# Two-part gather and weighting of expert tokens, with the adds moved behind the next block's first products

## The chip, the cores and the metric

One core of a Trainium2 chip runs the whole program. The metric is the device time of one execution in microseconds. Before the change three runs took 1808.55, 1808.65 and 1813.86 us, median 1808.65. A profile of one more execution (1807.88 us) was taken; all rows below are of that one.

## The reference

Two layers over 256 latent and 256 context tokens of width 1024. The change lies in the last stage, a mixture of experts over the 256 latent tokens, in float32 throughout:

```python
def moe_ffn(t, w_router, w1, w3, w2):
    logits = (t @ w_router).astype(jnp.float32)
    top_val, top_idx = lax.top_k(logits, TOP_K)
    gates = jax.nn.softmax(top_val, axis=-1)
    combine = jnp.sum(gates[..., None] * (top_idx[..., None] == jnp.arange(N_EXPERTS)), axis=-2)
    ...
    for e in range(N_EXPERTS):
        out = out + combine[..., e:e + 1] * swiglu(t, w1[e], w3[e], w2[e])
    return out
```

Each token takes two of eight experts (hidden width 3584). After it comes h = LayerNorm(sqrt(2) * h + mod5 * f), and that is the output.

## The kernel before, in words

The experts' stage is the last half of the program: from 878 us on the program loads 8 x 3 weight matrices, 352 MB, and ends some 20 us after the last of them. Tokens are sorted to experts on the chip. Experts are ranked by their number of tokens, and the rank fixes the room: 192, 128, 96, 96, 64, 32, 32 and 32 slots, 672 in all. `onehots` (L1467) builds two matrices G, 128 tokens x 672 slots, that hold 1 where a token sits in a slot. `gather` (L1491) multiplies the normalised rows n by G in two halves of 336 slots: for each of 8 feature blocks two float32 products, one for each half of the tokens; each result is scaled and shifted on its way out of PSUM and is the input xg of all experts. A float32 product appears in the trace as two records; a product of float32r operands, which `mm3` (L55) uses in the earlier stages, as one (a one-pass product in what follows). `split` (L49) makes such operands: ScalarE copies a tensor rounded to float32r, and VectorE subtracts the copy to get the rest.

The work is a list of jobs (`moe`, L1612): an expert's hidden width is cut in 7 chunks, and a chunk's slots in units of 128, 64 or 32 rows. `chunk_order` (L1582) interleaves chunks of large and of small experts. A job is `unit_hidden` (two products with the chunk's w1 and w3, then silu and product), `unit_turn` (a transpose, for units under 128 rows) and `unit_out` (the product with w2, added on VectorE to the unit's sum ya, tag "ya", 4 buffers). The order is `hidden(i)`, with the transposes of job i-1 inside it, then `out(i-1)`. Each chunk needs three loads of 2 MB, `wa`, `wb` and `wc` (L1602, L1605, L1608), from SyncE's queue into 7 buffers. A load waits in the queue until TensorE has finished with a buffer.

When an expert's last chunk is out, `unit_out` multiplies the sum by the row g5, `combine_matrix` (L1478) makes a slots x tokens matrix of gates (is-equal, times gate, transposed on TensorE, copied from PSUM at L1487), and `combine` (L1568) multiplies it with ya: four float32 products of 512 columns, each added to the residual rows K.res at L1576. There are 11 such units. The eleventh is of the expert that ends last; its last two chunks go through `ending` (L1679). The instructions of the loop are ordered by a planner that takes them in the program's order and moves ready ones forward on an idle engine; only `ending` and the router ahead of the stage stand in the written order. `overflow` (L1755) is a loop for tokens that found no slot; it runs zero times here. In `rest(0)` (L2154) two rows are spread over the partitions (L2147) and GpSimd makes K.res from n with them.

Of the kernel before, what the change touches and what calls it, by code (L numbers as in the profile page):

```python
# [1466 lines left out]
def onehots(K, pool, R):  # L1467
    nc = K.nc
    G = []
    for i in range(2):  # L1470
        G.append(pool.tile([128, NSLOT], F32, tag="ya", name="G", bufs=4))
        for r in range(NE):
            nc.vector.tensor_scalar(G[i][:, BASE[r]:BASE[r] + CAPS[r]], R.iota192[:, :CAPS[r]], R.pos[:, i, r:r + 1], None,
                                    op0=ALU.is_equal)
    return G


def combine_matrix(K, pool, R, kind, base, pos, gate, tag, bufs):  # L1478

    nc = K.nc  # L1480
    pt = K.bank()
    for i in range(2):
        t = pool.tile([128, 128], F32, tag="cmb_t", name="cmb_t", bufs=2)
        nc.vector.tensor_scalar(t, R.iot[(kind, base)], pos[:, i], gate[:, i], op0=ALU.is_equal, op1=ALU.mult)
        nc.tensor.transpose(pt[:, i * 128:(i + 1) * 128], t, K.ident)
    c = pool.tile([128, 256], F32, tag=tag, name="cmb", bufs=bufs)
    nc.vector.tensor_copy(c, pt[:, 0:256])  # L1487
    return c


def gather(K, n, G, lo, hi, xg, A, B):  # L1491
    nc = K.nc
    N = hi - lo
    for k in range(8):
        ps = K.bank()
        for i in range(2):
            nc.tensor.matmul(ps[:, :N], lhsT=n[i][:, k * 128:(k + 1) * 128], rhs=G[i][:, lo:hi], start=(i == 0), stop=(i == 1))  # L1497
        if k % 2:
            nc.scalar.activation(xg[:, k, lo:hi], ps[:, :N], AF.Identity, scale=A[:, k, 1:2], bias=B[:, k, 1:2])
        else:  # L1500
            nc.vector.tensor_scalar(xg[:, k, lo:hi], ps[:, :N], A[:, k, 1:2], B[:, k, 1:2], op0=ALU.mult, op1=ALU.add)
# [46 lines left out]
def unit_out(K, kind, gT, w2, ya, first, last):  # L1548
# [9 lines left out]
    for hf in range(2):  # L1558
# [3 lines left out]
        else:  # L1562
            K.nc.vector.tensor_tensor(ya[:, o], Y[hf], ya[:, o], op=ALU.add)  # L1563
        if last:
            K.nc.vector.tensor_tensor(ya[:, o], ya[:, o], K.g5[:, o], op=ALU.mult)  # L1565


def combine(K, c, ya):  # L1568

    nc = K.nc  # L1570
    for hf in range(2):
        o = slice(hf * 512, (hf + 1) * 512)
        for i in range(2):
            ps = K.bank()
            nc.tensor.matmul(ps, lhsT=c[:, i * 128:(i + 1) * 128], rhs=ya[:, o], start=True, stop=True)  # L1575
            nc.vector.tensor_tensor(K.res[i][:, o], ps, K.res[i][:, o], op=ALU.add)  # L1576


# [33 lines left out]
def moe(K, pool, R, G, n, A, B, rest):  # L1612
    nc = K.nc
    xg = pool.tile([128, 8, NSLOT], F32, tag="xg", name="xg")
    e = {}
    gather(K, n, G, 0, NSLOT // 2, xg, A, B)
    gather(K, n, G, NSLOT // 2, NSLOT, xg, A, B)
    ya = {}
    jobs = []

    def hidden(j, between=None):
# [10 lines left out]
    def out(j):  # L1632
        key = j["r"], j["u"]
        final = 4 if j["r"] == jobs[-1]["r"] else 6
        if j["ch"] == 0:
            ya[key] = pool.tile([128, D], F32, tag="ya", name="ya", bufs=4)
        if j["ch"] == final:
            r = j["r"]
            c = j["c"] = combine_matrix(K, pool, R, j["kind"], j["base"], R.pos[:, :, r:r + 1], R.gate[:, :, r:r + 1], "cmb", 2)
        unit_out(K, j["kind"], j["gT"], j["w"][2], ya[key], j["ch"] == 0, j["ch"] == final)  # L1640
        if j["ch"] == final:
            combine(K, c, ya.pop(key))

# [8 lines left out]
    for i in range(n - 2):  # L1652
        hidden(jobs[i], (lambda: turn(jobs[i - 1])) if i else None)
        if i:
            out(jobs[i - 1])
# [3 lines left out]
    turn(jobs[n - 3])  # L1659
    out(jobs[n - 3])  # L1660
    hidden(jobs[n - 2])
    return turn, hidden, jobs[n - 2:], jobs[n - 3]["c"]
# [91 lines left out]

def overflow(K, pool, R, n, A, B, end, nov):  # L1755
    nc = K.nc
    with K.tc.For_i(0, nov) as i:
# [4 lines left out]
        for t in range(2):  # L1762
            nc.vector.tensor_scalar(Gt[t], R.iot[(128, 0)], col[:, t:t + 1], None, op0=ALU.is_equal)
        xg = pool.tile([128, 8, 128], F32, tag="xg", name="ovx")
        gather(K, n, Gt, 0, 128, xg, A, B)
        c = combine_matrix(K, pool, R, 128, 0, col[:, 0:2, None], col[:, 2:4, None], "cmb", 2)
        ya = pool.tile([128, D], F32, tag="ya", name="ya", bufs=4)
        for ch in range(7):
            wa, wb, wc = load_chunk(K, e, ch)
            unit_out(K, 128, unit_hidden(K, pool, 128, xg, wa, wb)[0], wc, ya, ch == 0, ch == 6)  # L1770
        combine(K, c, ya)
        end()
# [21 lines left out]
def hybrid_block(ctx, tc, a, out, dbg=None, stop=None):  # L1794
# [30 lines left out]
    K.ph31 = cst.tile([128, 2, 64], F32, tag="ph31", name="ph31")  # L1825
    K.q_d = tc.dram_tile([16, 128, 240], F32, name="q_d")

    lnp = ctx.enter_context(tc.tile_pool(name="lnp", bufs=1))
# [150 lines left out]
    with tc.tile_pool(name="lat", bufs=1) as lp:  # L1979
# [10 lines left out]
        else:  # L1990
            n = latter(K, L, G, nn, lnp, sp, lp1, lp, ps, h[2:], g5)
    rn = ctx.enter_context(tc.tile_pool(name="rn", bufs=1))
    n2 = [rn.tile([128, D], F32, tag="n%d" % i, name="n") for i in range(2)]
# [142 lines left out]
    with tc.tile_pool(name="moew", bufs=1) as mw:  # L2136
        G = onehots(K, mw, R)

        row = [mo.tile([128, D], F32, tag="row%d" % i, name="row") for i in range(3)]

# [13 lines left out]
        def rest(i):  # L2154

            if i == 0:
                spread(0, row[0], ALPHA)
                spread(1, row[1], ALPHA)
# [14 lines left out]
        with tc.manual_schedule(engines=ALL):  # L2173
            ending(K, lnp, *lastly, row, out)
        overflow(K, mw, R, n, A2, B2, end, nov)

# [97 lines left out]
```

## Time and profile before

| | before |
|---|---|
| median of three runs | 1808.65 us |
| the profiled execution: its time, its span | 1807.88 us, 1806.0 us |
| TensorE busy, mean granted clock | 1690.3 us (94%), 0.970 |
| VectorE, ScalarE, GpSimd busy | 833.7, 408.8, 295.6 us |
| gather (L1497), 64 records | 882.2 to 902.3 us |
| combine products (L1575), 88 records | first at 1074.4, last at 1769.6 us |
| weight load queue | 509.5 MB, 73.6% of the 16 DMA engines' span |

Times in rows are microseconds from the start of the span, mean durations in ns. PE is TensorE's matmul, PEld its weight load, DVE is VectorE, ACT ScalarE, POOL GpSimd, SPq SyncE's queue. Matmuls overlap, so one record's duration is longer than the step from one to the next.

### The profile page before, as it was taken

The numbers are of one execution on the slowest core, as the hardware profiler recorded it, in microseconds if no ns is written. First come the engines' busy times: TensorE is split into PE (matmuls) and PEld (weight loads), VectorE is DVE, ScalarE is ACT, GpSimd is POOL, SyncE is SP. The second block draws the span as 40 slices with busy tenths as digits, with TensorE's granted clock in tenths as the row PEclk, the third lists the DMA queues.
The fourth block names the chain that finished last, engine by engine and source line by source line (L and its number), as shares of the span: only waits on it lengthen the run. The fifth ranks groups of instructions, "written<-read, shape, count | busy, mean of one in ns | idle before, by whom it ended". The sixth has DMA issues, their size and how long they took to land.

```text
span 1806.0 us, 34633 instructions
## 1 busy us (share of the span) xinstructions
PE 1690.3 (94%) x14673; PEld 1172.7 (65%) x14673; DVE 833.7 (46%) x1480; ACT 408.8 (23%) x775; POOL 295.6 (16%) x433
## 2 busy tenths in 40 slices
PE   6999997998999999559899999999999999999996
PEld 3755576776777777448576767666667665555553
DVE  2755559849987578994502121114011131241244
ACT  2555543222222464434210000000000001001001
POOL 7910005034542000563020000000000000000000
PEclk9999999999999999769989999999999999999998
DMA  8478762379996776868699799998999998999995
GB/s 322 163 244 264 260 193 92 117 201 283 308 301 220 251 250 200 252 170 311 279 400 401 312 400 396 427 426 351 373 426 396 397 390 327 427 426 376 390 388 212
DMA packets 96119, 556.29 MB, mean 308 GB/s; under 512 B 15128, under 2 KB 25052, under 8 KB 71128
## 3 DMA queue, kind: packets, MB, share of 16 engines
q1 hardware_dynamic: 78240, 509.52, 73.6%
q0 software_dynamic: 17536, 43.91, 8.4%
q8 instruction: 118, 1.93, 0.4%
q10 hardware_dynamic: 184, 0.59, 0.1%
q14 instruction: 41, 0.34, 0.1%
HBM read 529.41 MB, written 24.54 MB: 307 GB/s over the span
## 4 chain that ended last, share of the span: by engine, by line
PE 57%; DVE 6%; issue 2%; ACT 1%; POOL 1%; DMA 0%; ACTq 0%; DVEq 0%; POOLq 0%
PE bank L1526 18%; PE bank L1555 14%; PE bank L1517 11%; PE bank L57 2%; PE bank L58 2%; PE bank L59 2%; PE bank L1575 2%; PE bank L1497 1%; PE bank L1543 1%; DVE sG L1122 1%; PE bank L2147 1%; DVE su L1213 1%; ACT whl L51 0%; DVE ya L1563 0%; DVE ya L1565 0%
## 5 line engine op out<-in xcount | busy, mean ns | idle before, releaser
L1555 PE MATMUL bank<-wc,mgT 128*32 128x512 f32 (+2 forms) x1200 | 265.2, 598 | 0.5 <-DVE mgT L44 0.5
L1531 ACT ACTIVATE msl<-bank 128x128 f32<-128x128 f32 (+2 forms) x77 | 28.8, 374 | 730.9 <-PE bank L1526 558.9
L52 DVE TENSOR_TENSOR whl<-wraw,whl 128x1024 fp32r<-128x1024 f32 (+3 forms) x126 | 150.6, 1198 | 76.0 <-ACT whl L51 74.0
L1526 PE MATMUL bank<-wa,xg 128*32 128x128 f32 (+1 forms) x3136 | 173.7, 308 | 0.0
L59 PE MATMUL bank<-u,whl 128*128 128x512 f32 (+1 forms) x416 | 164.4, 395 | 9.6 <-DVE whl L52 9.6
L1526 PEld LDWEIGHTS bank<-wa,xg 128*32 128x32 f32 (+1 forms) x3136 | 125.9, 119 | 72.1 <-PE bank L1555 18.7
L1555 PEld LDWEIGHTS bank<-wc,mgT 128*32 128x32 f32 (+2 forms) x1200 | 85.6, 134 | 131.8 <-issue 127.2
L1526 PE MATMUL bank<-wb,xg 128*32 128x128 f32 (+1 forms) x3136 | 170.5, 304 | 0.0
L57 PE MATMUL bank<-u,whl 128*128 128x512 f32 (+1 forms) x416 | 166.6, 400 | 3.9 <-DVE u L52 3.9
L51 ACT CAST whl<-wraw 128x1024 fp32r<-128x1024 f32 (+3 forms) x126 | 125.6, 998 | 174.9 <-PE bank L59 142.5
L58 PE MATMUL bank<-u,whl 128*128 128x512 f32 (+1 forms) x416 | 163.7, 393 | 0.0
L1563 DVE TENSOR_TENSOR ya<-bank,ya 128x512 f32<-128x512 f32 x128 | 88.4, 690 | 139.4 <-PE bank L1555 139.2
L1532 DVE TENSOR_TENSOR msg<-msl,bank 128x128 f32<-128x128 f32 (+1 forms) x63 | 21.8, 347 | 270.9 <-PE bank L1526 270.9
L1526 PEld LDWEIGHTS bank<-wb,xg 128*32 128x32 f32 (+1 forms) x3136 | 122.2, 117 | 37.6 <-issue 3.7
L1746 POOL TENSOR_TENSOR y<-y,row 128x512 f32<-128x512 f32 x2 | 3.0, 1507 | 877.4 <-ACT y L1745 877.4
L1517 PEld LDWEIGHTS bank<-xg,wa 128*128 128x128 f32 x896 | 103.2, 194 | 9.0 <-PE bank L1555 6.0
L1517 PE MATMUL bank<-xg,wa 128*128 128x128 f32 x896 | 104.8, 279 | 0.0
L1517 PE MATMUL bank<-xg,wb 128*128 128x128 f32 x896 | 102.3, 275 | 0.0
L1517 PEld LDWEIGHTS bank<-xg,wb 128*128 128x128 f32 x896 | 101.2, 192 | 0.0
L59 PEld LDWEIGHTS bank<-u,whl 128*128 128x128 f32 x416 | 80.3, 193 | 29.1 <-DVE whl L52 11.3
L57 PEld LDWEIGHTS bank<-u,whl 128*128 128x128 f32 x416 | 80.6, 194 | 27.6 <-DVE u L52 4.7
L58 PEld LDWEIGHTS bank<-u,whl 128*128 128x128 f32 x416 | 80.3, 193 | 17.7 <-issue 0.8
(512 smaller groups left out, 2505.1 us busy)
## 6 DMA issues: line engine op xcount, KB each, us to landing
wa<-in_moe_w SPq DMA_DIRECT2D x56, 2048.0 KB, 10.2
wb<-in_moe_w SPq DMA_DIRECT2D x55, 2048.0 KB, 12.4
wc<-in_moe_w SPq DMA_DIRECT2D x55, 2048.0 KB, 14.3
wraw<-in_ffn_w SPq DMA_DIRECT2D x88, 512.0 KB, 4.8
adaw<-in_ada_w SPq DMA_DIRECT2D x80, 512.0 KB, 5.4
wraw<-in_w_o SPq DMA_DIRECT2D x16, 512.0 KB, 3.7
wf<-fs_d POOLq DMA_DIRECT2D x32, 256.0 KB, 9.5
wb<-in_s_bw POOLq DMA_DIRECT2D x32, 256.0 KB, 9.1
```

The lines of the kernel that those rows point to most:

```text
L51: K.nc.scalar.copy(hi, src)
L52: (eng or K.nc.vector).tensor_tensor(lo, src, hi.bitcast(F32), op=ALU.subtract)
L57: mm(ps, lhsT=l[0], rhs=r[1], start=start, stop=False)
L58: mm(ps, lhsT=l[0], rhs=r[0], start=False, stop=False)
L59: mm(ps, lhsT=l[1], rhs=r[0], start=False, stop=stop)
L1517: nc.tensor.matmul(p[:, b * 128:(b + 1) * 128], lhsT=w[:, k, b * 128:(b + 1) * 128], rhs=x[:, k, :], start=(k == 0), stop=(k == 7))
L1526: nc.tensor.matmul(p[kind * q:kind * (q + 1), :N], lhsT=x[:, k, :], rhs=w[:, k, q * N:(q + 1) * N], start=(k == 0), stop=(k == 7))
L1531: nc.scalar.activation(sl, p1[:, :N], AF.Silu)
L1532: nc.vector.tensor_tensor(g, sl, p3[:, :N], op=ALU.mult)
L1555: K.nc.tensor.matmul(Y[hf][kind * q:kind * (q + 1), :], lhsT=gT[:, b, kind * q:kind * (q + 1)], rhs=w2[:, q * nb + b, hf * 512:(hf + 1) * ...
L1563: K.nc.vector.tensor_tensor(ya[:, o], Y[hf], ya[:, o], op=ALU.add)
L1575: nc.tensor.matmul(ps, lhsT=c[:, i * 128:(i + 1) * 128], rhs=ya[:, o], start=True, stop=True)
```

## The change

Gather: n is split once into a rounded part nh and a rest nl (`split`, two calls of 128 x 1024), G is written as float32r (its ones are exact), and each of the 16 results is the sum of four one-pass products in place of two float32 ones. nh takes the place of two rows of `rest(0)`, nl two of the four "ya" buffers, until the gather is done.

Combine, for 10 of the 11 units: the matrix holds ones, not gates (a comparison with 0 in place of the copy), also float32r; a column reduction gives each slot's gate, and `unit_out` multiplies the sum by gate and g5 in one instruction. The sum is split in two halves of 512 columns, into tiles that take the place of n, and `combine` does two one-pass products for each result. The finished pair is put in a list, and `combine` runs after the `hidden` of the next iteration, ahead of its `out`. The eleventh unit keeps the float32 form.

Since the tiles of n are reused, n is also written to DRAM (two writes of 512 KB on GpSimd's queue in `rest(0)`), from where `overflow` would read it back. The diff without the lines of `overflow`:

```diff
@@ 
     for i in range(2):
-        G.append(pool.tile([128, NSLOT], F32, tag="ya", name="G", bufs=4))
+        G.append(pool.tile([128, NSLOT], F32R, tag="ya", name="G", bufs=4))
         for r in range(NE):
...
-def combine_matrix(K, pool, R, kind, base, pos, gate, tag, bufs):
+def combine_matrix(K, pool, R, kind, base, pos, gate, tag, bufs, ones=False):
@@ 
         nc.tensor.transpose(pt[:, i * 128:(i + 1) * 128], t, K.ident)
-    c = pool.tile([128, 256], F32, tag=tag, name="cmb", bufs=bufs)
+    c = pool.tile([128, 256], F32R if ones else F32, tag=tag, name="cmb", bufs=bufs)
+    if ones:
+        col = pool.tile([128, 1], F32, tag="gcol", name="gcol", bufs=2)
+        nc.vector.tensor_reduce(col, pt[:, 0:256], axis=AX.X, op=ALU.add)
+        nc.vector.tensor_scalar(c, pt[:, 0:256], 0.0, None, op0=ALU.is_gt)
+        return c, col
     nc.vector.tensor_copy(c, pt[:, 0:256])
...
 def gather(K, n, G, lo, hi, xg, A, B):
...
     nc = K.nc
...
         ps = K.bank()
-        for i in range(2):
-            nc.tensor.matmul(ps[:, :N], lhsT=n[i][:, k * 128:(k + 1) * 128], rhs=G[i][:, lo:hi], start=(i == 0), stop=(i == 1))
+        last = len(n[0]) * 2 - 1
+        for z, (i, x) in enumerate((i, x) for i in range(2) for x in n[i]):
+            nc.tensor.matmul(ps[:, :N], lhsT=x[:, k * 128:(k + 1) * 128], rhs=G[i][:, lo:hi], start=(z == 0), stop=(z == last))
         if k % 2:
@@ 
             K.nc.vector.tensor_tensor(ya[:, o], Y[hf], ya[:, o], op=ALU.add)
-        if last:
+        if last is True:
             K.nc.vector.tensor_tensor(ya[:, o], ya[:, o], K.g5[:, o], op=ALU.mult)
+        elif last is not None:
+            K.nc.vector.scalar_tensor_tensor(ya[:, o], ya[:, o], last, K.g5[:, o], op0=ALU.mult, op1=ALU.mult)
@@ 
             ps = K.bank()
-            nc.tensor.matmul(ps, lhsT=c[:, i * 128:(i + 1) * 128], rhs=ya[:, o], start=True, stop=True)
+            for z, y in enumerate(ya[hf]):
+                nc.tensor.matmul(ps, lhsT=c[:, i * 128:(i + 1) * 128], rhs=y, start=(z == 0), stop=(z == len(ya[hf]) - 1))
             nc.vector.tensor_tensor(K.res[i][:, o], ps, K.res[i][:, o], op=ALU.add)
...
+def halves(ya):
+    return [(ya[:, 0:512],), (ya[:, 512:1024],)]
@@ 
     e = {}
-    gather(K, n, G, 0, NSLOT // 2, xg, A, B)
-    gather(K, n, G, NSLOT // 2, NSLOT, xg, A, B)
+    nh = []
+    for i in range(2):
+        nh.append((K.mo.tile([128, D], F32R, tag="row%d" % i, name="nh"), pool.tile([128, D], F32R, tag="ya", name="nl", bufs=4)))
+        split(K, *nh[i], n[i])
+    gather(K, nh, G, 0, NSLOT // 2, xg, A, B)
+    gather(K, nh, G, NSLOT // 2, NSLOT, xg, A, B)
     ya = {}
     jobs = []
+    waiting = []
@@ 
         key = j["r"], j["u"]
-        final = 4 if j["r"] == jobs[-1]["r"] else 6
+        whole = j["r"] == jobs[-1]["r"]
+        final = 4 if whole else 6
+        last = None
         if j["ch"] == 0:
...
             r = j["r"]
-            c = j["c"] = combine_matrix(K, pool, R, j["kind"], j["base"], R.pos[:, :, r:r + 1], R.gate[:, :, r:r + 1], "cmb", 2)
-        unit_out(K, j["kind"], j["gT"], j["w"][2], ya[key], j["ch"] == 0, j["ch"] == final)
+            c = j["c"] = combine_matrix(K, pool, R, j["kind"], j["base"], R.pos[:, :, r:r + 1], R.gate[:, :, r:r + 1], "cmb", 2, not whole)
+            c, last = (c, True) if whole else c
+        unit_out(K, j["kind"], j["gT"], j["w"][2], ya[key], j["ch"] == 0, last)
         if j["ch"] == final:
-            combine(K, c, ya.pop(key))
+            y = halves(ya.pop(key))
+            if not whole:
+                for hf in range(2):
+                    p = K.rn.tile([128, 2, 512], F32R, tag="n%d" % hf, name="yh")
+                    split(K, p[:, 0], p[:, 1], y[hf][0])
+                    y[hf] = p[:, 0], p[:, 1]
+            waiting.append((c, y))
@@ 
         hidden(jobs[i], (lambda: turn(jobs[i - 1])) if i else None)
+        while waiting:
+            combine(K, *waiting.pop())
         if i:
@@ 
     out(jobs[n - 3])
+    while waiting:
+        combine(K, *waiting.pop())
     hidden(jobs[n - 2])
@@ 
     K.q_d = tc.dram_tile([16, 128, 240], F32, name="q_d")
+    K.n_d = tc.dram_tile([2, 128, D], F32, name="n_d")
@@ 
             n = latter(K, L, G, nn, lnp, sp, lp1, lp, ps, h[2:], g5)
-    rn = ctx.enter_context(tc.tile_pool(name="rn", bufs=1))
+    rn = K.rn = ctx.enter_context(tc.tile_pool(name="rn", bufs=1))
     n2 = [rn.tile([128, D], F32, tag="n%d" % i, name="n") for i in range(2)]
@@ 
-        row = [mo.tile([128, D], F32, tag="row%d" % i, name="row") for i in range(3)]
+        row = {2: mo.tile([128, D], F32, tag="row2", name="row")}
@@ 
             if i == 0:
+                for t in range(2):
+                    GP.dma_start(K.n_d[t], n[t])
+                    row[t] = mo.tile([128, D], F32, tag="row%d" % t, name="row")
                 spread(0, row[0], ALPHA)
```

## Rows read from the trace of the kernel before

**Rows 1.** The page: busy tenths in 40 slices of 45 us, and DMA's.

```profile
PE   6999997998999999559899999999999999999996
DMA  8478762379996776868699799998999998999995
```

**Rows 2.** Waits, TensorE from 878 us: line, waited for, us in total, times, longest.

```profile
PE bank L1575 <- DVE ya L1565: 8.1, 11, 0.9
PE bank L1497 <- DVE G L1473: 5.4, 1, 5.4
```

**Rows 3.** Waits of SyncE's DMA queue from 900 us, the longest sum.

```profile
SPq L1602 <- PE bank L1555: 284.1, 21, 21.2
```

**Rows 4.** Windows: length, busy us (records) per engine, PEclk, DMA share, GB/s.

```profile
876.00:880.00 4.00, 0.80 (x8) 0.71 (x7) 3.27 (x18) 0.22 (x1) 0.00 (x0) 0.85 0.59 175
...
882.00:884.00 2.00, 1.81 (x3) 1.00 (x4) 2.00 (x14) 0.00 (x0) 0.00 (x0) 0.50 1.02 434
884.00:886.00 2.00, 2.00 (x5) 1.20 (x4) 1.34 (x5) 0.00 (x0) 0.00 (x0) 0.59 0.97 410
886.00:906.00 20.00, 20.00 (x187) 14.21 (x186) 4.38 (x7) 6.61 (x10) 0.00 (x0) 1.00 1.01 431
...
1105.00:1200.00 95.00, 95.00 (x1096) 68.26 (x1089) 15.43 (x27) 4.89 (x13) 0.00 (x0) 1.00 1.00 424
```

**Rows 5.** The chain that ended last, around combines: start, length, what.

```profile
1228.93 1.89 PE bank L1526 x64
...
1233.43 2.75 PE bank L1555 x12
...
1237.68 3.70 PE bank L1575 x8
1241.38 7.14 PE bank L1517 x64
...
1499.23 3.59 PE bank L1555 x16
```

**Rows 6.** Timeline of TensorE, one-pass products of 512 columns: start, length, record.

```profile
834.03 0.39 PE L58 MATMUL bank<-wg,zT 128*128 128x512 f32 x1
834.26 0.39 PE L59 MATMUL bank<-wg,zT 128*128 128x512 f32 x1
```

**Rows 7.** Groups by line and shape: count, busy us, mean ns, idle before.

```profile
L52 DVE TENSOR_TENSOR whl<-wraw,whl 128x1024 fp32r<-128x1024 f32 x106 | 134.0, 1266 | 57.8 <-ACT whl L51 55.9 <-PE bank L272 1.8
L52 DVE TENSOR_TENSOR lows<-qkf,kn 128x512 fp32r<-128x512 f32 x8 | 5.7, 708 | 3.4 <-ACT kn L51 3.4
L51 ACT CAST kn<-qkf 128x512 fp32r<-128x512 f32 x8 | 5.0, 621 | 16.5 <-DVE qkf L299 16.5
```

**Rows 8.** Timeline, gather to the third job's first product: start, length, records.

```profile
881.34 2.86 DVE L1473 TENSOR_SCALAR G<-rc,pos 128x192 f32<-128x192 f32 x16
...
882.18 20.12 PE L1497 MATMUL bank<-G,n 128*128 128x336 f32 x64 [5.38 <-DVE G L1473]
...
916.90 7.41 PE L1517 MATMUL bank<-xg,wa 128*128 128x128 f32 x64
```

**Rows 9.** Two single weight loads, issue and landing: sixth and eighth.

```profile
L1608 SPq DMA_DIRECT2D wc<-in_moe_w x1: 333/333/333, 881.6 to 881.6; - x1
DMA to landing us min/median/max: 29.9/29.9/29.9
...
L1605 SPq DMA_DIRECT2D wb<-in_moe_w x1: 333/333/333, 904.3 to 904.3; - x1
DMA to landing us min/median/max: 17.2/17.2/17.2
```

**Rows 10.** The last `wa` load, and in the chain its first use.

```profile
L1602 SPq DMA_DIRECT2D wa<-in_moe_w x1: 338/338/338, 1759.5 to 1759.5; - x1
DMA to landing us min/median/max: 13.9/13.9/13.9
...
1779.28 1.88 PE bank L1526 x64
```

More of the change, by code (lines that the diff above doesn't have):

```diff
@@ L1752, in ending, with overflow @@
             A.copy(K.res[i][:, O[x]], P[i][x])
-def overflow(K, pool, R, n, A, B, end, nov):
+def overflow(K, pool, R, A, B, end, nov):
     nc = K.nc
@@ L1763, in overflow @@
             nc.vector.tensor_scalar(Gt[t], R.iot[(128, 0)], col[:, t:t + 1], None, op0=ALU.is_equal)
+        n = [K.rn.tile([128, D], F32, tag="n%d" % t, name="n") for t in range(2)]
+        for t in range(2):
+            nc.sync.dma_start(n[t], K.n_d[t])
         xg = pool.tile([128, 8, 128], F32, tag="xg", name="ovx")
-        gather(K, n, Gt, 0, 128, xg, A, B)
+        gather(K, [(x,) for x in n], Gt, 0, 128, xg, A, B)
         c = combine_matrix(K, pool, R, 128, 0, col[:, 0:2, None], col[:, 2:4, None], "cmb", 2)
@@ L1769, in overflow @@
             wa, wb, wc = load_chunk(K, e, ch)
-            unit_out(K, 128, unit_hidden(K, pool, 128, xg, wa, wb)[0], wc, ya, ch == 0, ch == 6)
-        combine(K, c, ya)
+            unit_out(K, 128, unit_hidden(K, pool, 128, xg, wa, wb)[0], wc, ya, ch == 0, True if ch == 6 else None)
+        combine(K, c, halves(ya))
         end()
@@ L2156, in rest @@
             if i == 0:
+                for t in range(2):
+                    GP.dma_start(K.n_d[t], n[t])
+                    row[t] = mo.tile([128, D], F32, tag="row%d" % t, name="row")
                 spread(0, row[0], ALPHA)
@@ L2174, in hybrid_block @@
             ending(K, lnp, *lastly, row, out)
-        overflow(K, mw, R, n, A2, B2, end, nov)
+        overflow(K, mw, R, A2, B2, end, nov)
 def _tokens(x):
```

## The prediction

> **What bounds the kernel now.** I read the page's slices first. In the experts' half, slices 20 to 39, TensorE is at 9 tenths almost throughout, and so are the DMA engines [rows 1]: two resources run near full beside each other, and which of them ends a stage has to be read in that stage. The waits tell it. From 878 us TensorE waits 8.1 us for the gated sum ahead of the 11 combines and 5.4 us for the matrices G ahead of the gather, and for no weight load [rows 2]. SyncE's queue on the other hand waits for TensorE to give up buffers, 284.1 us in its largest group alone [rows 3]. So as a whole TensorE ends the stage. Two places look different in the windows: from 882 to 906 us, and from 1105 to 1200 us, the DMA engines have no room left at 410 to 434 GB/s [rows 4]. Where TensorE becomes faster there, the weights may be what is late.
>
> **The combines.** The chain of waits gives a combine's price. From a unit's output products to the next block's first product it is 1241.38 - 1233.43 = 7.95 us where a combine stands between, and 3.59 us for the same 16 records where none does: 4.36 us [rows 5]. Counted the other way: eight records in 3.70 us, and 8.1 / 11 = 0.74 us of wait before them, together 4.44 us [rows 2, 5]. I take 4.4. After the change the same four results need eight one-pass records. Their step at full clock is 834.26 - 834.03 = 0.23 us [rows 6], so 1.85 us. The wait goes if the finished pair is ready when the next block's first products are through. Behind the last output product stand, on VectorE, two adds, two gated multiplies and two subtractions of 512 columns at about 0.7 us (4.2 us, the first add overlapping), and on ScalarE two copies of 0.62 us between them [rows 7]: the pair is ready some 3.5 to 4 us after the last product. The shortest block that can cover it is a 32-row unit, two passes of 1.89 us [rows 5], 3.8 us, and a short transpose between them. Four of the ten pairs have such a short cover; the others have 7 us and more. Without the cover TensorE would wait those 4 us. I take 2.5 us saved for each of ten: 25 us. Bounds for each: 4.4 - 1.85 = 2.55, and 2.55 - 4 = -1.5 with no cover at all. The eleventh combine is not changed. The extra VectorE work (two subtractions, a reduction, a comparison for a copy, some 1.8 us a unit) lies beside products: VectorE is busy a sixth of the stage [rows 4]. What is late next after a combine is the next block, whose weights have long landed in most places (below).
>
> **The gather itself.** Now 64 records take 20.12 us from 882.18 [rows 8], the first of them at half clock: 0.50 is granted from 882 to 884 us and 0.59 to 886, after TensorE had stood idle, which costs 1.0 + 0.8 = 1.8 us [rows 4]. After: 64 one-pass records of 336 columns, 336/512 of 0.23 us, 9.7 us. They start later, since the first result needs both parts of both halves. G ends at 881.34 + 2.86 = 884.2 [rows 8], two subtractions of 1024 columns behind it take 1.27 us each [rows 7], so steady work from 886.7; with the same 1.8 us for the clock it ends at 898.2, 4 us earlier than 902.3. If the subtractions slip into the gaps ahead of G it is 6.6 us; if the clock stays low throughout, 4 us later than now. ScalarE's copies find that engine idle.
>
> **Where those 4 us go.** Job 0 and 1 get them, job 2 does not. Its `wa` is the seventh load. The sixth landed at 881.6 + 29.9 = 911.5, the eighth at 904.3 + 17.2 = 921.5 [rows 9], in a stretch where the DMA engines are full, so the seventh landed about 916.5. TensorE took it up at 916.90 [rows 8]: the two met already. Coming 4 us earlier it waits 4 us. The gather's gain is at most 0.4 us here, and the ~10 us of records saved are off the path.
>
> **What the early part loses.** First, the two writes of n, 1.05 MB, are new traffic: 2.4 us at 431 GB/s if they fall into the full stretch, nothing if they fit in before. From 876 to 880 us the engines are 0.59 busy [rows 4], 1.6 us of room; the second half of n is ready at about 876, the weights start at 878.5. I take 0.7 us of delay to the seventh load, 917.2, 0.3 us later than job 2 begins now. Second, TensorE stands idle some 4 to 5 us ahead of job 2, about as long as ahead of the gather, where the clock then was low for 1.8 us' worth of work [rows 4]. I charge the same 1.8 us to job 2; bounds 0 and twice that. Together 2.1 us lost, between a gain of 0.4 and a loss of 5.6.
>
> On these two, two rules of the Trainium skill. DMA: Bandwidth & Descriptors, section "Issuing engines are not separate DMA queues", says that transfers of all issuing engines share the same 16 DMA engines, so a write from GpSimd's queue takes the weights' place. By it the whole 2.4 us come off, and the time is 1.7 us more than mine. TensorE: Matmul & The Clock Gate, Part 1, says that the clock follows how busy TensorE has lately been. The fall to 0.50 after an idle stretch agrees, and without the rule the sum would be 1.8 us less.
>
> **Does the rest of the gain get through the weights?** Between 1105 and 1200 us both resources are full [rows 4]. The first combine (at 1074) shortens TensorE by 2.5 us ahead of that stretch; the loads move along, since they are issued when TensorE gives up buffers [rows 3], and the put-off combine lets two buffers go earlier still. From 1210 on nine combines follow, and the DMA engines have gaps. At the end the last `wa` lands at 1759.5 + 13.9 = 1773.4 and is first used at 1779.28 [rows 10], 5.9 us of cover. The two combines just before (5 us) speed TensorE but not the already full queue, so 0.9 us is left: enough, and no more.
>
> **Sum.** 25 - 2.1 = 22.9 us. The profiled execution, 1807.88 us (span 1806.0), becomes 1785.0; it stands 0.8 us below the median of the runs shown, which becomes 1785.8. I predict 1786.
>
> **Rivals.**
> A. The weights do not bind at job 2, since the seventh load's landing is inferred from its neighbours: the gather's 4 us stay and nothing is lost early, 1808.65 - 25 - 4 = 1780. Against it: its two neighbours landed 10 us apart, the time of two loads.
> B. The cover is too short in part: four pairs with a 32-row block wait 2 us each, and the others lose half a us to bank or VectorE order: 22.9 - 8 - 3 = 12 us, 1797. For it: 3.8 us of cover against 3.5 to 4.
> C. The weights bind more widely: what is saved up to 1200 us and in the last two combines comes back as waits for loads, and only seven combines count, with a third of each lost again where light chunks follow, and the early part costs its full 5.6 us: 7 x 2.5 x 2/3 - 5.6 = 6 us, 1803. For it: DMA share 1.00 up to 1200 us; against it: 5.9 us of cover at the end.
> D. Slower: the planner puts the adds directly behind their unit, not behind the next block, because it takes the split for short. Then TensorE waits out the split at each unit: 1.85 + 4 us plus the pair's second half on VectorE, 0.7, is 6.5 against 4.4, ten times 2.1, with the 2.1 us of the early part: 1832. It decides from the point where the wait passes 2.55 us a unit; with 3 us it would be 1815. Against it: the program's own order has `hidden` first, and those instructions are ready.
> That the change does not do what it says, the one-pass products costing as much as float32, is ruled out by the 0.23 us step in a stage where one weight load goes with each product [rows 6].
>
> **How the numbers follow.** Forecast 0.66, A 0.08, B 0.12, C 0.09, D 0.05. The range takes in the forecast with its bounds (early part +0.4 to -5.6, combines 2.2 to 2.55 us each: 1783 to 1792), A at its lower end and B at its upper: 1780 to 1797, which leaves out C and D and half of A and B's tails. About 0.3%, 5.4 us, is what a measurement of this kernel can tell from no change. Forecast, A, B and half of C are faster by more than that: 0.90. The other half of C and a part of D's near end lie within: 0.06. Slower: 0.04.
>
> **What would show it.** Right: gather records of 0.15 us steps ending near 898; a wait of TensorE of 4 to 5 us for `wa` at about 912 to 917, and a low granted clock just after it; job 2 beginning within 1 us of 916.9, or later; combine records in 1.9 us directly behind a block's w3 products, with less than 0.3 us of wait for the split; each combine moving the later work by 2.5 us; the last blocks' weights landing less than 1 us ahead of use. Wrong: job 2 beginning at 913 (A); waits of L1575 on VectorE's subtraction over 1 us (B, D); waits on `wa` or `wb` after 1200 us (C).

## The result and the profile after

The changed kernel takes 1781.13 us (median of 4 runs, 1779.93 to 1784.2) against 1808.6 us (median of 4, 1803.52 to 1813.86): a ratio of 0.985, 95% interval 0.9819 to 0.9882. Measured again later, in 6 runs, it is 1784.34 against 1805.03 us, 0.9888 (0.9865 to 0.9911). The forecast was 1786 us. The profiled execution after took 1779.93 us, its span is 1778.1 us.

Lines have moved: the gather is L1504, the hidden products L1524 (128-row units) and L1533 (64 and 32 rows), the output products L1562, the combine L1585, the weight loads L1616, L1619 and L1622. TensorE's waits from 870 us (line, what it waited for, us in total, times, longest), to be read beside [rows 2]:

```profile
PE bank L1504 <- DVE G L1473: 5.5, 1, 5.5
PE bank L1524 <- DMA wa<-in_moe_w: 5.1, 2, 4.9
...
PE bank L1585 <- DVE ya L1572: 0.7, 1, 0.7
```

The 8.1 us in front of the combines are 0.7 us now, all of it at the eleventh, which was not changed. No wait of a combine for its split is listed. New is a wait of 4.9 us for the weights of job 2. Where it lies is seen in the timeline of TensorE (start, length, records; the gather's last record, job 0, the end of job 1, job 2) and answers to [rows 8]:

```profile
892.08 0.32 PE L1504 MATMUL bank<-G,nl 128*128 128x336 f32 x1
892.33 1.41 PE L1533 MATMUL bank<-wa,xg 128*32 128x128 f32 x44
...
906.71 1.89 PE L1562 MATMUL bank<-wc,mgT 128*32 128x512 f32 x16
913.51 10.20 PE L1524 MATMUL bank<-xg,wa 128*128 128x128 f32 x64 [4.91 <-DMA wa<-in_moe_w]
```

The chain of waits around one combine (start, length, what), as in [rows 5]:

```profile
1218.16 1.88 PE bank L1533 x64
1220.04 0.37 PE bank L1550 x2
1220.41 1.88 PE bank L1533 x64
1222.30 2.05 PE bank L1585 x8
```

Eight one-pass records in 2.05 us stand directly behind the next block's w3 products. And the single loads and writes that [rows 9] and [rows 10] were about (issue, landing): the first weight load, the two writes of n, the sixth load, the last `wa`.

```profile
L1616 SPq DMA_DIRECT2D wa<-in_moe_w x1: 368/368/368, 875.2 to 875.2; - x1
...
L2194 POOL DMA_DIRECT2D n_d<-n x2: 563/570/578, 866.0 to 873.3; - x2
DMA to landing us min/median/max: 2.9/3.0/3.0
...
L1622 SPq DMA_DIRECT2D wc<-in_moe_w x1: 333/333/333, 878.3 to 878.3; - x1
DMA to landing us min/median/max: 30.2/30.2/30.2
...
L1616 SPq DMA_DIRECT2D wa<-in_moe_w x1: 338/338/338, 1728.9 to 1728.9; - x1
DMA to landing us min/median/max: 20.1/20.1/20.1
```

**Where the 27.95 us between the two profiled executions come from.** I cut each span at the issue of the first weight load: what lies ahead is code that the change leaves alone but for the two writes of n, what lies behind is the experts' stage. Before: 1806.0 = 878.5 + 927.5. After: 1778.1 = 875.2 + 902.9. So 24.6 us come from the stage, where the prediction had put 22.9, and 3.3 us from ahead of it. Over the fourteen profiles of this study the first load is issued anywhere from 874.0 to 883.1 us, twice in the same kernel at 875.2 and 879.8. The kernel of before with its float32 combines put off has 874.8 without any write of n. So the 3.3 us are not shown to be a gain of the change. Below, "stage" is the span less the first issue.

Inside the stage, counted from the first issue: job 0 begins at 17.1 us in place of 23.7, job 2 at 38.3 as before (38.4), job 6 at 90.1 in place of 90.6. Then the ten combines move the rest by 2.46 us each on average, and the end comes 24.6 us earlier. By the medians the whole program gains 27.5 us and, measured again, 20.7 us.

### The profile page after: what moved, and what is told of

It is laid out like the page before. It is cut to its first block, busy times and chain, and to the rows that moved or that the text cites. A ratio compares the mean times of both kernels' runs of the same rounds, so it can differ in the third digit from the quotient of the medians.

```text
span 1778.1 us, 34698 instructions
## 1 busy us (share of the span) xinstructions
PE 1661.8 (93%) x14673; PEld 1169.3 (66%) x14673; DVE 849.8 (48%) x1512; ACT 423.3 (24%) x797; POOL 296.9 (17%) x435
## 4 chain that ended last, share of the span: by engine, by line
PE 54%; DVE 5%; DMA 4%; issue 2%; ACT 1%; POOL 1%; SPq 0%; ACTq 0%; POOLq 0%; DVEq 0%
PE bank L1533 18%; PE bank L1562 14%; PE bank L1524 12%; DMA wa<-in_moe_w 3%; PE bank L57 2%; PE bank L58 2%; PE bank L59 2%; PE bank L1585 1%; PE bank L1550 1%; DMA wraw<-in_ffn_w 1%; DVE sG L1122 1%; ACT whl L51 1%; DMA wgr<-in_w_glu 0%; DVE su L1213 0%; DMA sph<-ph_d 0%
## 5 line engine op out<-in xcount | busy, mean ns | idle before, releaser
L1562 PE MATMUL bank<-wc,mgT 128*32 128x512 f32 (+2 forms) x1200 | 265.0, 597 | 0.5 <-DVE mgT L44 0.5
L1562 PEld LDWEIGHTS bank<-wc,mgT 128*32 128x32 f32 (+2 forms) x1200 | 85.6, 134 | 131.5 <-issue 125.9
L1533 PEld LDWEIGHTS bank<-wa,xg 128*32 128x32 f32 (+1 forms) x3136 | 125.1, 119 | 71.0 <-PE bank L1562 19.2
L1533 PE MATMUL bank<-wa,xg 128*32 128x128 f32 (+1 forms) x3136 | 171.8, 307 | 0.0
L1533 PE MATMUL bank<-wb,xg 128*32 128x128 f32 (+1 forms) x3136 | 171.3, 306 | 0.0
L1533 PEld LDWEIGHTS bank<-wb,xg 128*32 128x32 f32 (+1 forms) x3136 | 122.9, 118 | 37.8 <-issue 3.7
L1524 PEld LDWEIGHTS bank<-xg,wa 128*128 128x128 f32 x896 | 106.0, 199 | 14.5 <-issue 7.6
L1524 PE MATMUL bank<-xg,wa 128*128 128x128 f32 x896 | 107.6, 283 | 5.1 <-DMA wa<-in_moe_w 5.1
L1524 PE MATMUL bank<-xg,wb 128*128 128x128 f32 x896 | 102.3, 275 | 0.0
L1524 PEld LDWEIGHTS bank<-xg,wb 128*128 128x128 f32 x896 | 101.2, 192 | 0.0
```

The lines of the kernel that those rows point to most:

```text
L1524: nc.tensor.matmul(p[:, b * 128:(b + 1) * 128], lhsT=w[:, k, b * 128:(b + 1) * 128], rhs=x[:, k, :], start=(k == 0), stop=(k == 7))
L1533: nc.tensor.matmul(p[kind * q:kind * (q + 1), :N], lhsT=x[:, k, :], rhs=w[:, k, q * N:(q + 1) * N], start=(k == 0), stop=(k == 7))
L1562: K.nc.tensor.matmul(Y[hf][kind * q:kind * (q + 1), :], lhsT=gT[:, b, kind * q:kind * (q + 1)], rhs=w2[:, q * nb + b, hf * 512:(hf + 1) * ...
```

## The experiments

The stage repeats far better than the whole time (902.9 and 902.8 in the two profiles of the changed kernel, 927.5 and 927.6 in those of before; 899.9 and 903.0 in those of combine_only are the exception, taken up there), so I give both. "TensorE's clock" below is the granted clock.

| kernel | first weight issue | stage | ratio to before, 95% |
|---|---|---|---|
| before, twice | 878.5, 878.2 | 927.5, 927.6 | 1 |
| changed, twice | 875.2, 879.8 | 902.9, 902.8 | 0.985, 0.9888 (intervals above) |
| gather_only | 877.0 | 925.6 | 1.0014 (0.9997 to 1.0031) |
| combine_only, twice | 876.4, 877.7 | 899.9, 903.0 | 0.9863 (0.9838 to 0.9888), 0.9835 (0.9813 to 0.9858) |
| put_off_float32 | 874.8 | 917.2 | 0.9946 (0.9928 to 0.9964) |
| combine_not_put_off | 874.6 | 941.3 | 1.0079 (1.0054 to 1.0105) |
| fill_the_wait | 874.0 | 901.3 | 0.9876 (0.9852 to 0.9899) |
| heavy_first / with float32 gather | 875.3 / 875.8 | 903.5 / 913.5 | 0.9901 (0.9873 to 0.9929) / 0.9936 (0.9913 to 0.9958) |
| heavy_second / with float32 gather | 883.1 / 881.0 | 895.6 / 904.3 | 0.9847 (0.9816 to 0.9877) / 0.9858 (0.9834 to 0.9883) |

The theory: all of the gain is in the ten combines, and the gather's is swallowed because job 2's weights land no earlier. The rivals: the gather carries part of it; putting off alone, or the parts alone, carry the combines' share.

**The gather alone.** The changed kernel with the combine of before:

```
-            c = ...combine_matrix(..., "cmb", 2, not whole)
+            c = j["c"] = combine_matrix(..., "cmb", 2)
 ...
-                    split(K, p[:, 0], p[:, 1], y[hf][0])
 ...
-            waiting.append((c, y))
+            combine(K, c, halves(ya.pop(key)))
```

> The new gather with the combines of before (float32, gates in the matrix, run directly behind the unit's last products). Theory (the weights of job 2 bind, so an earlier gather is swallowed): the gather ends about 6 us earlier after the first weight load is issued than in before, TensorE then waits about 5 us for the `wa` of job 2 in place of none to 1 us, job 2 begins 38 to 39 us after the first weight issue as in before, and the time stays within 2 us of before: 1806 to 1811 us. Rival 1 (the gather's gain passes on to the end): 1802 to 1803 us. Rival 2 (the early losses that the prediction counted, 2.1 us from the clock and the two writes of the rows): 1810 to 1811 us, with the low clock in job 2's first products and nothing given back by job 4.

Measured 1804.46 against 1802.8 us, 1.0014 (0.9997 to 1.0031): no gain is seen. TensorE's waits have one row for weights:

```profile
PE bank L1524 <- DMA wa<-in_moe_w: 5.9, 1, 5.9
```

Job 0 begins 17.6 us after the first issue, 6 us earlier than before, and job 2 at 38.1 us, where it always began. The theory holds and rival 1 falls. The loss of rival 2 is not in the stage, which is 1.9 us shorter than before; 1.5 us of that are the clock's (next experiment). The interval of the times doesn't exclude it.

**The combines alone.** The float32 gather of before in the changed kernel:

```
-        G.append(pool.tile([128, NSLOT], F32R, ...
+        G.append(pool.tile([128, NSLOT], F32, ...
 ...
-    nh = []
-    for i in range(2):
 ...
-        split(K, *nh[i], n[i])
+    nh = [(x,) for x in n]
```

> The new combines (parts with exact ones, two passes, put off) with the float32 gather of before. Theory (all of the gain is in the ten combines): as the changed kernel, 24 to 25 us below before, 1782 to 1786 us, and job 2 begins 38 to 39 us after the first weight issue without a wait of more than 2 us. Rival (the gather carries part of it): about 6 us slower than the changed kernel, 1788 to 1790 us.

Measured 1777.94 against 1802.8 us, 0.9863: 24.7 us by the ratio, all of the gain. The stage, 899.9 us, is even 3.1 us shorter than with the split gather. Whether that is a price of the split gather or chance was open, so it ran again beside other kernels:

> The new combines with the float32 gather, again, beside the others. Theory (the split gather costs 2 to 3 us in the changed kernel, by the wait and the lower clock behind it): 899 to 901 us from the first weight issue to the end against 902.9 of the changed kernel, and 0.985 to 0.988 of before. Rival (the difference between the two was the chip's): 902 to 904 us.

0.9835 by the times, but a stage of 903.0 us: here the rival came in. The two profiles of one kernel differ as much as the two kernels did, and the granted clock says why. Two windows of each profile, 38.2 to 68.2 us and 120 to 145 us behind the first issue (length, then busy us and records of the five engines, granted clock, DMA share, GB/s). The first combine_only:

```profile
914.61:944.61 30.00, 30.00 (x231) 22.43 (x229) 3.28 (x11) 2.92 (x6) 2.57 (x2) 1.00 1.01 423
996.41:1021.41 25.00, 25.00 (x224) 21.36 (x223) 1.96 (x4) 3.57 (x7) 0.00 (x0) 0.93 0.68 286
```

The second:

```profile
915.91:945.91 30.00, 30.00 (x215) 22.03 (x213) 2.07 (x3) 2.92 (x6) 1.04 (x1) 0.89 0.96 398
997.71:1022.71 25.00, 25.00 (x263) 20.28 (x262) 3.34 (x6) 3.63 (x7) 0.00 (x0) 0.93 0.82 343
```

The changed kernel:

```profile
913.43:943.43 30.00, 29.92 (x215) 23.86 (x216) 2.07 (x3) 2.33 (x5) 0.00 (x0) 0.90 0.95 397
995.23:1020.23 25.00, 25.00 (x265) 20.46 (x264) 3.29 (x6) 3.63 (x7) 0.00 (x0) 0.93 0.80 335
```

Before:

```profile
916.74:946.74 30.00, 30.00 (x213) 22.02 (x211) 2.07 (x3) 2.94 (x7) 1.17 (x1) 0.89 0.95 395
998.54:1023.54 25.00, 25.00 (x261) 20.15 (x261) 3.34 (x6) 3.63 (x7) 0.00 (x0) 0.93 0.82 346
```

TensorE is busy throughout these windows, so the share of the clock that is missing times the length is time lost: 1.75 us in the first combine_only, 3.3 + 1.75 = 5.05 us in the second, 4.75 in the changed kernel, 5.05 before. In gather_only it is 3.55 us (0.94 and 0.93). Taken off the stages, the two combine_only profiles stand at 898.1 and 898.0 us, the changed kernel at 898.1, before at 922.5 and gather_only at 922.0. What is left of the change is 24.4 us in ten combines, 2.44 us each, and the split gather is worth nothing here, for or against, as far as the clock's share is no part of it. Where the clock falls differs between two profiles of one kernel. One of the places hangs on the wait for job 2's weights, as "Filling the wait" below shows.

**Putting off alone.** Before with its float32 combine moved, nothing else:

```
-            combine(K, c, ya.pop(key))
+            waiting.append((c, ya.pop(key)))
 ...
+        while waiting:
+            combine(K, *waiting.pop())
         if i:
             out(jobs[i - 1])
 ...
     out(jobs[n - 3])
+    while waiting:
+        combine(K, *waiting.pop())
     hidden(jobs[n - 2])
```

> The kernel of before with one edit: its float32 combines, with the gates in the matrix, are put off behind the next block's first products; no parts, float32 gather. Theory: putting off takes away only the wait for the gate (8.1 us in 11 combines, 0.74 each) and leaves four float32 products of 3.7 us: ten times 0.7 is 7 us, 1800 to 1803 us. Rival 1 (the order carries all of it, the parts nothing): 1782 to 1787 us. Rival 2 (the wait comes back somewhere else, the products of the next block wait for banks or weights): 1807 to 1811 us.

Measured 1793.34 against 1802.8 us, 0.9946: 9.7 us by the ratio (6.5 to 13), where the theory said 7 and rivals 1 and 2 nearly all or nothing. The chain shows a combine without a wait before it, in float32:

```profile
1220.70 1.88 PE bank L1526 x64
1222.58 3.63 PE bank L1575 x8
```

Eight records in 3.63 us and no wait, against 4.4 before. The same two windows as above:

```profile
912.99:942.99 30.00, 30.00 (x232) 22.24 (x228) 2.75 (x8) 2.92 (x6) 2.54 (x2) 1.00 1.00 418
994.79:1019.79 25.00, 25.00 (x221) 20.83 (x212) 1.96 (x4) 3.63 (x7) 0.00 (x0) 0.86 0.74 302
```

The clock cost 3.5 us here and 5.05 before. Without it the stages are 913.7 and 922.5: 8.8 us, 0.88 us a combine, of which the wait of [rows 2] is 0.74 and the products 0.07 (3.70 and 3.63). The other part of the 2.44 us is 1.56, and 3.63 - 2.05 = 1.58 is what the parts save in the chains: the two add up.

**The parts without putting off.**

```
-            waiting.append((c, y))
+            combine(K, c, y)
```

> The changed kernel with each combine run directly behind its unit's last products and split, as before's was, not behind the next block's first products. Theory (the split is on the path when the combine isn't put off; this is the price of rival D): TensorE waits 2.5 to 4.7 us per unit for the split, less what the planner moves ahead of it, so a combine costs 4.4 to 6.5 us in place of the 1.9 us of the changed kernel and the 4.4 us of before: 1808 to 1830 us, no faster than before. Rival (the two passes alone carry the gain, putting off is worth nothing): 1782 to 1787 us with waits below 0.3 us.

Measured 1818.18 against 1802.8 us, 1.0079 (1.0054 to 1.0105): slower than before, by 15.4 us by the medians, between the 6 and the 23 us that rival D of the prediction gave. TensorE's waits have this row:

```profile
PE bank L1585 <- ACT yh L51: 20.6, 18, 2.2
```

and the chain shows what stands in front of a combine:

```profile
1223.07 0.70 DVE ya L1570
...
1223.80 0.76 DVE ya L1574
...
1224.58 0.63 ACT yh L51
...
1225.23 0.69 DVE yh L52
1225.92 0.67 DVE ya L1574
...
1226.62 0.63 ACT yh L51
...
1227.29 0.73 PE bank L1585 x2
1228.02 0.79 PE bank L1533 x24
1228.81 0.66 PE bank L1585 x2
```

From the last output product (1223.05) the chain of add, gate, copy and, for the second half, gate and copy again takes 4.24 us to 1227.29. On VectorE the second half's gate (1225.92) begins where the first half's subtraction ends (1225.23 + 0.69). Only the last two of the eight products got work of the next block ahead of them. So a combine costs 38.4 / 10 = 3.8 us more than put off (stages 941.3 and 902.9) and 1.4 more than before's (927.5).

Most of that 1.4 is the clock. It was 0.81 over the 30 us from 912.81, 0.93 over the 25 us from 994.61, and 0.83, 0.88 and 0.83 over 10, 28 and 10 us from 1072, 1466 and 1760; TensorE was busy wherever it was low, so 14.2 us were lost. Without them the stage is 927.1 us: 2.9 us a combine more than put off (898.1) and 0.5 more than before's (922.5). The last three stretches lie at combines that waited for their split; no other profile with this order of the chunks has a low clock between 150 us behind the first issue and its last product.

The parts save 1.6 us a combine only because the put-off time covers those 4.24 us. In the chain after, five of the ten pairs are covered by a 32-row unit: 1.88 + 0.37 + 1.88 = 4.13 us at 1218.16, between 3.63 and 4.03 us at the others. At the shortest the combine begins with the half that is ready first, and the second half's subtraction ends 0.5 us behind that:

```profile
1452.46 3.63 PE bank L1533 x128
...
1455.85 0.69 DVE L52 TENSOR_TENSOR yh<-ya,yh 128x512 fp32r<-128x512 f32 x1 [0.69 <-ACT yh L51]
1456.02 2.12 PE L1585 MATMUL bank<-yh,cmb 128*128 128x512 f32 x8
```

**Filling the wait at job 2.** Five float32 products of 512 columns, not used, ahead of job 2:

```
+        if i == 2:
+            ps = K.bank()
+            for z in range(5):
+                nc.tensor.matmul(ps, lhsT=xg[:, z, 0:128], rhs=xg[:, z, 128:640], start=True, stop=True)
         hidden(jobs[i], ...
```

> The changed kernel with five float32 products of 512 columns on tokens already gathered, their result not used, ahead of job 2, where TensorE waited 4.9 us for the weights (five at about 0.86 us are 4.3 us). Theory (the wait is what brings the lower clock in job 2's first products, which took 10.2 us there and 7.3 us in kernels without the wait): job 2's `wa` products take 7.3 to 7.6 us, job 4 begins 2.8 us earlier after the first weight issue (73.9 against 76.65), and it is still there at the end: 2 to 3 us faster than the changed kernel. Rival 1 (the clock falls at this place whatever TensorE does): job 2 at 10 us, same time as the changed kernel. Rival 2 (the filler delays job 2): up to 1 us slower.

The timeline shows the filler and job 2's `wa` products:

```profile
906.62 4.56 PE L1684 MATMUL bank<-xg 128*128 128x512 f32 x10
912.17 7.38 PE L1524 MATMUL bank<-xg,wa 128*128 128x128 f32 x64 [0.99 <-DMA wa<-in_moe_w]
```

7.4 us, not 10.2, and the wait 1.0 us in place of 4.9. The stage is 901.3 us, 1.6 less than the changed kernel, not 2.8, since the clock fell for longer near 130 us (0.86 over the 25 us from 994.04, in place of 0.93). By the times it is 0.9876 against 0.9888 for the changed kernel beside it: not told apart.

How the wait and the clock go together is seen in windows of the first 10.8 us of job 2, of the changed kernel, of this one and of before, and of before's next 15 us:

```profile
913.43:924.23 10.80, 10.72 (x71) 10.75 (x72) 0.00 (x0) 0.48 (x1) 0.00 (x0) 0.72 1.01 426
...
912.24:923.04 10.80, 10.80 (x97) 10.80 (x98) 0.00 (x0) 0.75 (x2) 0.00 (x0) 1.00 1.00 426
...
916.74:927.54 10.80, 10.80 (x99) 10.64 (x96) 0.00 (x0) 1.36 (x4) 1.17 (x1) 1.00 1.00 425
927.54:942.54 15.00, 15.00 (x83) 8.74 (x83) 2.07 (x3) 1.19 (x2) 0.00 (x0) 0.81 1.01 428
```

Ten profiles have this order of the chunks. In the four in which TensorE waited 4.9 us or more for these weights the clock is low in these 10.8 us: 0.72 and 0.86 in the changed kernel, 0.83 in gather_only, 0.79 in combine_not_put_off. In the six others (before twice, combine_only twice, put_off_float32 and this kernel) it is 1.00. So at this place the theory holds: the low clock comes with the wait, and it is gone where the wait is filled. It cost 3.0 us in the first profile of the changed kernel and 1.5 in the second; with the wait filled job 4 begins 73.7 us behind the first issue in place of 76.65. But before and the second combine_only lost 3.3 us a little later in jobs that had no wait, and the first combine_only did not. What decides that fall stays open, and with it whether the split gather costs a little by the clock or not.

> The changed kernel itself, beside the others. Theory: the ten combines give 24 to 25 us, and the split gather gives nothing or costs up to 3 us (TensorE's wait for job 2's weights is followed by a stretch at the lower clock): 0.985 to 0.988 of before, at or up to 3 us behind the same kernel with the float32 gather (0.9863). Rival (the gather's gain reaches the end after all): 0.982 to 0.984.

0.9888 is at the edge of what the theory gave, and its interval (0.9865 to 0.9911) leaves out the rival (0.982 to 0.984).

**An order in which the weights don't bind at job 2.** If only the early weights swallow the gather, it must count where they don't. One number in the order of the chunks, so that the heavy expert's first chunk goes first:

```
-        x = heavy.pop(0) if heavy and (pe <= 0.9*dma-12 or not light) else light.pop(0)
+        x = heavy.pop(0) if heavy and (pe <= 0.9*dma or not light) else light.pop(0)
```

> The changed kernel with one number in the order of the chunks: a chunk of the heavy expert goes first (where estimated work is at or below 0.9 of estimated loading, not 12 us below it). Job 0 then runs for some 25 us on one chunk while four more loads land. Theory (the first loads, not the gather, set when the light chunks could run): no wait for weights over 1 us in the first 60 us after the first weight issue, and the early end of the gather counts; from the durations of the phases and a load every 4.9 us into seven buffers I work out 10 us less than the changed kernel from the first weight issue to the end: 890 to 896 us in place of 902.9, so 1768 to 1775 us where the changed kernel has 1780. Rival 1 (the loads bind over the whole stage, only the place of the wait moves): same as the changed kernel within 2 us. Rival 2 (the light chunks are missing later where the heavy ones ran beside them, and TensorE waits at the end): slower by 3 to 10 us.

> The same order with the float32 gather of before. Theory (weights do not bind at the first jobs in this order, so here the gather's speed counts): 5 to 7 us slower than the same order with the split gather, and the whole difference stands at job 2 already. Rival (the gather's gain is swallowed in any order): within 2 us of it, or faster by up to 3 us as the float32 gather keeps the clock up.

No gain over the changed kernel: 0.9901 against 0.9888, stage 903.5 against 902.9. My estimate of 10 us was wrong; it had the output products of a 128-row unit at 3.5 us where the trace has 7.0. The place of the wait moved, as rivals 1 and 2 said, to the end, where the last chunks' loads are late (TensorE's waits from 1600 us):

```profile
PE bank L1724 <- DMA wc<-in_moe_w: 3.1, 2, 1.9
PE bank L1533 <- DMA wb<-in_moe_w: 2.7, 1, 2.7
PE bank L1533 <- DMA wa<-in_moe_w: 1.9, 1, 1.9
```

But the float32 gather is behind in this order: 913.5 against 903.5 us of stage, 1792.78 against 1785.65 us in time (the two intervals against before overlap, so this rests on the stage). Job 0 begins 6.5 us later and job 2 too (58.7 against 52.2 us). Most of the other 3.5 us is the clock: the float32 kernel has 0.98 over the 70 us from 930 and 0.94 over the 30 us from 1000, 3.2 us in all, where the other has 1.00. With 6 in the place of 12 (one light chunk, then the heavy one):

> The changed kernel with 6 us in place of 12 in the order of the chunks: one light chunk, then the heavy expert's first. Sized anew from the phases in the traces (7.4, 7.2 and 7.0 us for a 128-row unit; the working of the run with the heavy chunk first had its last phase at half): no wait for weights at the first two chunks, then about 2 us at five places as now, and the end is not bound by loads more than now: 5 to 6 us less than the changed kernel from the first weight issue to the end, 896 to 898 us; 0.985 to 0.986 of before. Rival 1 (as with the heavy chunk first: what is won at the start is lost in a wait for the last chunks' loads): 901 to 904 us. Rival 2 (the loads bind at the second heavy chunk instead): 900 to 903 us, with one wait of 3 us or more at job 5.

> The same order with the float32 gather. Theory: in this order the gather's end sets when the first two chunks run, so this is 6 to 8 us behind the same order with the split gather. Rival (weights swallow the gather here too): within 2 us of it.

The stage is 895.6 us, 7.3 less than the changed kernel and the shortest of all; no wait for weights over 1 us is left:

```profile
PE bank L1724 <- DMA wc<-in_moe_w: 0.9, 1, 0.9
```

Of the 7.3 us some are the clock's. It was low here only ahead of 921 us and at the end, from 921.31 to 1764.40 it is 1.00. The low stretch inside the jobs:

```profile
900.11:916.11 16.00, 16.00 (x194) 14.59 (x194) 0.34 (x2) 4.58 (x7) 9.29 (x4) 0.79 1.01 430
```

That is 3.4 us, here with no wait behind it that would swallow them. Without them the stage is 892.2 against 898.1 us: the order is worth 5.9 us, as the working (5 to 6) had it.

With the float32 gather it is 904.3, 8.7 more, 7.0 of it at the first product already (23.9 against 16.9 us). So the theory holds in two orders by the stage: where the weights don't bind at the first heavy chunk, the split gather's 6.5 to 7 us count. The times of the second pair do not settle it: 0.9847 and 0.9858 differ by 2 us, with intervals of 5 us on either side, and both profiles have a late first weight issue (883.1 and 881.0). Nor do the times show heavy_second ahead of combine_only (0.9835 and 0.9863). It beats before; that it beats the changed kernel is shown for the stage alone.

> The kernel of before, one look on this chip. Theory (its first stage differs from run to run by some us, and so does where the clock falls; the stage behind it is the same): the first weight load issued anywhere from 874 to 880 us, and 924.5 to 927.6 us from there to the end, the lower end if the clock does not fall in jobs 1 to 3.

As the theory had it: first issue at 878.2, stage 927.6 us, the clock falling where it fell in the first profile.

## Why the prediction was right, point by point

- **What bounds.** Right: two stretches with full DMA engines, and in the first of them the weights took over (DMA share 1.01 in the window where job 2 begins, behind a wait of 4.9 us).
- **The combines, 25 us.** Right: 24.4 us with the clock taken off. One product is 0.26 us on average in the chain (2.05 / 8), not 0.23, and the wait was 0.74 as read. The cover was as tight as I had it, 3.63 us at the shortest for a pair ready after some 4.1, and held because half a pair is enough to begin. That was not in the prediction, which asked for the whole pair. Five pairs have so short a cover, not four.
- **The gather swallowed.** Right, and the central point: job 2 unmoved, 38.3 against 38.4 us. How much the gather gained was off: 4 us were counted and 6.6 came. That is the figure of the second case given, but the case itself, subtractions in the gaps ahead of G, did not happen; the number is luck. They stood behind G, 1.21 us each, and ended 7.9 us behind the first issue, where 8.2 was counted. What the sum had left out is that eight products with nh (the rounded part) began before the subtractions, and that TensorE went on with the first nl (the rest) and did not wait for the second:

```profile
878.04 2.86 DVE L1473 TENSOR_SCALAR G<-rc,pos 128x192 fp32r<-128x192 f32 x16
...
879.00 2.58 PE L1504 MATMUL bank<-G,nh 128*128 128x336 f32 x8 [5.51 <-DVE G L1473]
880.82 2.35 DVE L52 TENSOR_TENSOR nl<-n,nh 128x1024 fp32r<-128x1024 f32 x2
...
882.09 0.65 PE L1504 MATMUL bank<-G,nl 128*128 128x336 f32 x1 [0.52 <-DVE nl L52]
```

- **The early part, a loss of 2.1 us.** Wrong: the stage shows none. For the writes 0.7 us was counted. They were issued at 866.0 and 873.3 and landed 3 us later, ahead of the weights or beside the first; the sixth load landed 33.3 us after the first issue against 33.0 before. The Trainium skill's rule (DMA: Bandwidth & Descriptors, "Issuing engines are not separate DMA queues") was given its full price of 2.4 us there as a case; the trace shows no conflict, because the writes hardly met the loads. For the clock 1.8 us was counted at job 2, and there the loss came: 0.72 over 10.8 us is 3.0 us, 0.86 in the second profile 1.5. What failed is that I added it to what before lost. Before had lost 3.3 us to a low clock in its third and fourth job, where the changed kernel lost nothing behind job 2's first products; with the fall near 130 us it is 5.05 us before and 4.75 after. Nothing in the prediction said that the two would cancel; that they did is luck. The Trainium skill's other rule, that the clock follows TensorE's recent busyness (TensorE: Matmul & The Clock Gate, Part 1), agrees with the low clock behind the 4.9 us wait; before's own fall stands in a window in which TensorE was busy for 30.00 of 30.00 us.
- **Does the rest get through.** Right: the last `wa` landed at 1749.0 and was used at 1750.8, 1.8 us of cover where I had 0.9, and no wait for `wa` or `wb` after 1200 us is among those over 0.4 us.
- **The sum.** For the profiled execution 1785.0 was predicted and 1779.9 measured: 3.3 us are the first weight issue's, which is not shown to be the change's, and 1.7 the stage's, about the early loss of 2.1 that was none, less the 0.6 that the combines gave under 25. That the median, 1781.13, came out lower than forecast is thus in part luck; measured again the gain by the medians is 20.7 us, 2 less than forecast.
- **The rivals.** A fell: job 2 began at 38.3 us. B and C fell: no wait for the split, none for weights of note after job 2. D did not happen, and its price lay between the two figures given: run at once, the combine gives 1818 us where before takes 1803.

## What to carry to other kernels

Cut a span at a fixed event before comparing: here the part ahead of the change moved by 9 us between profiles, the stage behind it by 0.1 us in the same kernel with the same loss to the clock. A faster step in front of a full queue was worth nothing here until the order of the work behind it was changed; ask for the landing of the load that the next large job needs. Splitting for cheaper products and putting them off belong together: the first without the second made this kernel slower (1.0079), the second alone gave 9.7 us.

## What the hardware showed

- A one-pass product of 512 columns steps at 0.23 to 0.26 us and one of 336 columns at 0.15 us (891.78 to 891.93 in the gather); the same result in float32 costs two records, 3.63 us for four results against 2.05 with two parts.
- The granted clock fell to half at different places in two profiles of one kernel with the same stage code, worth 3.1 us of stage (899.9 and 903.0), as much as several of the effects studied here.
- With a wait of 4.9 us or more ahead of job 2 the granted clock was 0.72 to 0.86 in the 10.8 us behind it (four profiles), without it 1.00 (six profiles, one of them with the wait filled by unused products).
